# Loading the experts' weights one expert at a time in 8192-byte pieces

## The chip, the cores and the metric

The kernel runs on one core of a Trainium2 chip. A core has a matrix engine (PE), a vector engine (DVE), a scalar engine (ACT), a general engine (POOL), a queue that issues most transfers (SP) and 16 DMA engines that carry them between HBM and the on-chip memory of 128 partitions. The metric is the time of one execution in device microseconds, as a median of three runs.

## What is computed

A block of a network on 512 tokens of width 1024, all in float32: a mixer (a gated recurrence beside a spatial gating unit), and then a mixture of 32 experts of which each token takes two. The change touches the second half:

```python
mod = silu(c) @ ada_w + ada_b
sh1, sc1, g1, sh2, sc2, g2 = split(mod, 6)          # 1024 columns each
...
h = rmsnorm(x, norm2_g) * (1 + sc2) + sh2           # the second norm, modulated
g_logits = h @ w_grp + b_grp                        # 4 groups
e_logits = h @ w_exp + b_exp                        # 32 experts
# for each token the two best experts of its best group, with weights
y = (silu(h @ w1[e]) * (h @ w3[e])) @ w2[e]         # w1, w3: 1024 x 512; w2: 512 x 1024
x = rmsnorm(x + g2 * sum(weight * y), final_g)
```

The weights of 32 experts are 3 x 2 MB each, 192 MB, and every one of them is read once.

## The kernel before

The tokens lie in four tiles of 128 partitions. **The front** (to about 235 us) normalizes x, forms the modulation, runs the mixer, adds it to x (x2), turns x2 for the router's logits, ranks the tokens by expert and gathers the first ones. **The experts** are then worked through in 13 blocks of two or four experts (BLOCKS): each expert has 32 to 96 of the 128 columns of a block, and a block with two experts runs as [w1 and w3 of both, then w2 of both]. Between those products PE gathers the tokens of later blocks (lines 946 and 817), makes the one-hot matrices and adds the results of the block before to x2 (line 960).

**The modulation** comes in 12 units of 512 columns (class Ada). Units 6 to 9 are those of the second norm; each takes 256 columns of the shift and 256 of the scale, so its weights come in rows of 256 numbers, four transfers of 512 KB for a unit. unit.mm() multiplies them with silu(c), ACT copies the result from PSUM (line 208), columns() turns it into columns with four small products (line 215), and modulate() adds the bias and multiplies with the gain. Of the second norm's columns the program keeps an order of its own: x's column 256 k + 2 c + i stands in partition c of column 2 k + i. paired() is that view (every second column), parity() its other side; gain, bias and the router's weights are loaded in the same order: gain and bias into rows_b with 4-byte elements (line 260), the router's weights into wr (lines 302 and 303).

**The order of columns** has one purpose: with it a partition's rows of w1 are neighbours in memory. rows_of() gives w1 and w3 as `(k p i) f -> p k (i f)` with i = 2, that is, two rows of 512 numbers, 4096 bytes in one piece; a row of w2 has 1024 numbers, 4096 bytes too.

**The loads** are all on SP's queue in the order in which they are written. An experts' tile is 8 KB in each partition, 1 MB in all; it holds the same piece of two experts, each filled by a transfer of its own (512 KB, line 1056). The tiles stand in a ring of 12 buffers (RING: five w8, one l8, two w8q, four w8r); the first 14 loads take the buffers as the front lets them go (FIRST). A transfer waits until the buffer's last reader is done, and each transfer has one of eight semaphores in turn, so it waits as well for the transfer eight places before it. In block 0 the order is: w3, the first tile of w1, w2, two tiles of block 1's w1, the rest of w1, then the rest of block 1's w1 and its w3. Then the queue comes to a branch (line 1268) that leaves out the work for tokens that no block has room for, and goes on with block 1's w2. In the last block w2 comes in parts of 256 columns (LAST), in pieces of 1024 bytes.

**The products** of a block: up() runs k = 0 to 7 and within it the experts, so step k needs row chunk k of every expert in the block; mm() runs q = 0 to 3, both halves of the output, and the experts. In the front and in the blocks PE's order is the written one in part and a scheduler's in part; SP's is always the written one.

Of the kernel before, what the change touches and what calls it, by code (L numbers as in the profile page):

```python
# [15 lines left out]
P = 128  # L16
# [29 lines left out]
def trunk(ctx, tc, a, out):  # L46
# [132 lines left out]
    class Ada:  # L179


        def __init__(self, pieces):
            self.pieces = pieces
# [26 lines left out]
        def columns(self, second):  # L210

            ps = bank("m", (P, 4))
            for q in range(4):
                m = paired(self.m)[:, q // 2, q % 2] if second else self.m[:, q * P:(q + 1) * P]
                pe.matmul(ps[:, q:q + 1], m, quad[:, 0:1], start=True, stop=True)
            return ps
# [29 lines left out]
    unit += [Ada((3072 + 256 * q, 4096 + 256 * q)) for q in range(4)]  # L246
# [109 lines left out]
    def cg(name, k):  # L356
        return cols_g[:, off[name] + k:off[name] + k + 2]
# [34 lines left out]
    def modulate(u, q, s):  # L392
        second = s is s2c
        ps = u.columns(second)
        t = small.tile([P, 2], F32, name="modt")
        gain, shift, scale = (cg(name, 8 * i + 2 * q) if second else ca(name, 8 * i + 2 * q, 2)
                              for name, i in ((("g2n", 0), ("ada2", 0), ("ada2", 1)) if second else
                                              (("g1n", 0), ("ada", 0), ("ada", 1))))
        dve.scalar_tensor_tensor(t, ps[:, 2:4], 1.0, scale, op0=OP.add, op1=OP.add)
        dve.tensor_tensor(s[:, 1, 2 * q:2 * q + 2], ps[:, 0:2], shift, op=OP.add)  # L400
        dve.tensor_tensor(s[:, 0, 2 * q:2 * q + 2], t, gain, op=OP.mult)
# [60 lines left out]
    modulate(unit[0], 0, s1)  # L462
# [9 lines left out]
    modulate(unit[1], 1, s1)  # L472
# [4 lines left out]
    modulate(unit[2], 2, s1)  # L477
# [12 lines left out]
    modulate(unit[3], 3, s1)  # L490
# [127 lines left out]
    modulate(unit[6], 0, s2c)  # L618
# [16 lines left out]
    for k in range(KD):  # L635
        proj_step(b_u, k, ps)
        if k % 2 == 1:
            split_to(29 + k)
        if k == 1:
            unit[8].mm()  # L640
            unit[9].mm()
        if k == 4:
            modulate(unit[7], 1, s2c)
        if k == 6:
            modulate(unit[8], 2, s2c)
# [36 lines left out]
    def chunk(k):  # L682

        return slice((k % 2) * 512 + (k // 2) * P, (k % 2) * 512 + (k // 2 + 1) * P)
# [4 lines left out]
    def turned(hf, t):  # L689
# [11 lines left out]
    for k in range(KD):  # L701
# [6 lines left out]
        if k == 2:  # L708
            modulate(unit[9], 3, s2c)
# [32 lines left out]
    def logits(t, hf):  # L742
# [11 lines left out]
        act.activation(nh[:, t, :].rearrange("p (i m) -> p i m", i=2), parity(x2[:, t, :]), AF.Copy, scale=r)  # L754
# [25 lines left out]
    def parts(t, eng=None):  # L780
        for hf in range(2):
            cs = slice(hf * 512, (hf + 1) * 512)
            lo, hi = [v[:, t].rearrange("p (i h m) -> p h i m", i=2, h=2)[:, hf] for v in (nl, nh.bitcast(F32))]
# [239 lines left out]
    def rows_of(src, f):  # L1023

        i = D // f
# [4 lines left out]
    class Weights:  # L1030
# [3 lines left out]
        def __init__(self, name, b, f, cs=None, n=1):  # L1034
# [13 lines left out]
            self.todo = [(j, k) for k in range(0, self.src[0].shape[1], n) for j in range(0, len(self.src), 2)]  # L1048

        def load(self, most=2 * KD):  # L1050

            for q in range(min(most, len(self.todo))):
                j0, k = self.todo.pop(0)
                t = slot8((P, 2, self.n, self.src[0].shape[2]))
                for j in range(2):
                    sync.dma_start(t[:, j], self.src[j0 + j][:, k:k + self.n])
                    w = t[:, j] if self.cs else t[:, j].rearrange("p k (i f) -> p (k i) f", f=self.f)
                    self.r[j0 + j] += [w[:, q, :] for q in range(w.shape[1])]
# [16 lines left out]
    def block(b, along, early, before_y, after):  # L1075
# [62 lines left out]
        gT = hidden_t(gt)  # L1138
# [39 lines left out]
    def over_block(number):  # L1178
# [9 lines left out]
        def weights(src, k):  # L1188
            t = t2((P, 512))
            sync.dma_start(t, src[:, k // 2, (k % 2) * 512:(k % 2 + 1) * 512])  # L1190
# [215 lines left out]
```

## Time and profile before

| | us |
|---|---|
| median of three runs | 733.29 (731.32 to 733.75) |
| the profiled execution | 730.36 |
| its span, first to last instruction | 728.6 |
| PE busy | 678.5 (93%) |
| DVE busy | 295.6 (41%) |
| ACT busy | 174.8 (24%) |

The rows below come from the profiled execution, times in it are counted from the start of its span. An engine's busy time is the time that its instructions ran; matmuls overlap, so PE's share says little about how full it is. Of more use is the chain that ended last: it goes back from the last instruction, at each step to what released it.

### The profile page before, as it was taken

What the parts mean: (1) busy time and instruction counts of PE and PEld (TensorE: products, weight loads), DVE (VectorE), ACT (ScalarE), POOL (GpSimd) and SP (SyncE); (2) the same over time, 40 slices, a digit from 0 to 9 for tenths busy, and PEclk for the clock granted to TensorE, in tenths of its full rate; (3) what the DMA queues carried; (4) which work ended last, traced back from release to release, by engine and by line L of the source; (5) the groups of instructions that cost most, each with busy time, mean ns of one, the idle gap of its engine ahead of it and who ended that gap; (6) DMA issues with size and microseconds to landing.
All of it is one profiled execution on the core that took longest, in us unless ns stands there. A gap on an engine that the chain in (4) does not pass through costs nothing.

```text
span 728.6 us, 10224 instructions
## 1 busy us (share of the span) xinstructions
PE 678.5 (93%) x3693; PEld 358.9 (49%) x3693; DVE 295.6 (41%) x690; ACT 174.8 (24%) x317; POOL 24.4 (3%) x55
## 2 busy tenths in 40 slices
PE   8799999999998999999999999989899999989873
PEld 6467766767887435432544444333144544442131
DVE  7459439452568823311333332221123322333025
ACT  5244496342344210100110110100001110111014
POOL 3000000000103000000000000000000000000011
PEclk9899999999999999999999999999999999999997
DMA  8999606885629869999999999999999999999993
GB/s 293 287 347 319 231 1 208 274 306 208 244 78 338 346 249 409 408 409 410 408 409 409 408 410 409 409 410 408 408 410 408 409 410 408 409 404 409 361 328 118
DMA packets 99487, 246.33 MB, mean 338 GB/s; under 512 B 14072, under 2 KB 40296, under 8 KB 99432
## 3 DMA queue, kind: packets, MB, share of 16 engines
q1 hardware_dynamic: 98152, 245.09, 88.6%
q8 instruction: 30, 0.49, 0.3%
q10 hardware_dynamic: 1056, 0.52, 0.3%
q14 instruction: 25, 0.20, 0.1%
q0 software_dynamic: 224, 0.02, 0.0%
HBM read 243.51 MB, written 2.10 MB: 337 GB/s over the span
## 4 chain that ended last, share of the span: by engine, by line
DMA 60%; PE 29%; DVE 4%; SPq 3%; ACT 3%; issue 1%; POOL 0%; DVEq 0%; ACTq 0%
DMA w8r<-in_expert_w 20%; DMA w<-in_expert_w 18%; DMA l<-in_expert_w 18%; PE h L1104 4%; PE c L437 3%; PE h L437 3%; PE y L1151 3%; PE y L437 2%; PE m L204 2%; DMA w<-in_ada_w 2%; SPq L260 1%; PE h L90 1%; PE h L91 1%; PE m L946 1%; PE h L92 1%; DMA sbb<-in_sgu_b 1%
## 5 line engine op out<-in xcount | busy, mean ns | idle before, releaser
L1104 PE MATMUL h<-w,l 128*64 128x512 f32 (+1 forms) x608 | 135.5, 598 | 5.1 <-DMA w<-in_expert_w 5.0
L961 DVE TENSOR_TENSOR x<-x,c 128x512 f32<-128x512 f32 x96 | 65.9, 686 | 39.4 <-PE c L960 39.4
L1104 PEld LDWEIGHTS h<-w,l 128*64 128x64 f32 (+1 forms) x608 | 37.1, 125 | 89.5 <-issue 56.6
L1104 PE MATMUL h<-w8r,l 128*32 128x512 f32 (+1 forms) x304 | 61.9, 598 | 2.8 <-DMA w8r<-in_expert_w 2.8
L960 PE MATMUL c<-l,cT 128*128 128x512 f32 x192 | 62.4, 406 | 0.0
L946 PE MATMUL m<-l,b16h 128*128 128x256 f32 (+1 forms) x192 | 51.8, 294 | 3.2 <-ACT l L817 3.1
L1151 PE MATMUL y<-w8q,gT 128*64 128x512 f32 (+2 forms) x240 | 50.0, 570 | 3.9 <-DMA w8q<-in_expert_w 2.3
L985 DVE TENSOR_TENSOR t<-y,g2b 128x512 f32<-128x512 f32 x24 | 16.6, 692 | 89.8 <-PE y L1151 88.5
L86 ACT ACTIVATE l<-t 128x512 fp32r<-128x512 f32 (+1 forms) x35 | 21.3, 613 | 130.3 <-DVE t L985 115.7
L1151 PE MATMUL y<-w8r,gT 128*64 128x512 f32 (+2 forms) x240 | 49.3, 566 | 3.2 <-DMA w8r<-in_expert_w 3.2
L1131 DVE SCALAR_TENSOR_TENSOR t<-t,ws,h 128x512 f32<-128x512 f32 x13 | 9.7, 747 | 98.6 <-PE h L1104 98.6
L946 PE MATMUL m<-l,b16l 128*128 128x256 f32 (+1 forms) x192 | 49.1, 279 | 0.0
L817 ACT ACTIVATE l<-m,s2c 128x256 f32<-128x256 f32 (+1 forms) x24 | 13.1, 547 | 147.6 <-PE m L946 147.6
L946 PEld LDWEIGHTS m<-l,b16h 128*128 128x128 f32 x192 | 36.1, 188 | 19.6 <-ACT l L817 8.3
L242 DVE TENSOR_TENSOR w8r<-w,w8r 128x512 fp32r<-128x512 f32 x48 | 30.7, 685 | 26.6 <-ACT w8r L240 26.6
L1104 PEld LDWEIGHTS h<-w8r,l 128*32 128x32 f32 (+1 forms) x304 | 16.3, 120 | 44.8 <-issue 26.0
L946 PEld LDWEIGHTS m<-l,b16l 128*128 128x128 f32 x192 | 36.3, 189 | 2.5
L240 ACT ACTIVATE w8r<-w 128x512 fp32r<-128x512 f32 x48 | 26.9, 621 | 33.5 <-PE h L92 17.6
L1122 DVE SCALAR_TENSOR_TENSOR ws<-m,of 128x4 f32<-128x4 f32 (+1 forms) x13 | 2.1, 163 | 80.1 <-PE m L1119 80.1
L437 PE MATMUL c<-b16h,w8r 128*128 128x512 f32 x80 | 31.2, 414 | 3.1 <-ACT b16h L406 2.6
L960 PEld LDWEIGHTS c<-l,cT 128*128 128x128 f32 x192 | 29.2, 189 | 6.7 <-issue 3.4
L1114 ACT ACTIVATE t<-h 128x512 f32<-128x512 f32 x13 | 7.8, 598 | 99.4 <-PE h L1104 99.4
(358 smaller groups left out, 953.8 us busy)
## 6 DMA issues: line engine op xcount, KB each, us to landing
w<-in_expert_w SPq DMA_DIRECT2D x160, 512.0 KB, 10.1
w8r<-in_expert_w SPq DMA_DIRECT2D x124, 512.0 KB, 10.2
w8q<-in_expert_w SPq DMA_DIRECT2D x64, 512.0 KB, 10.2
l<-in_expert_w SPq DMA_DIRECT2D x36, 512.0 KB, 10.3
w<-in_ada_w SPq DMA_DIRECT2D x32, 512.0 KB, 7.5
w<-in_w_in SPq DMA_DIRECT2D x8, 1024.0 KB, 8.9
w<-in_ada_w SPq DMA_DIRECT2D x8, 1024.0 KB, 11.1
w<-in_w_out SPq DMA_DIRECT2D x4, 1024.0 KB, 8.8
```

The source lines that it names most:

```text
L86: act.activation(hi, src, AF.Copy)
L204: pe.matmul(self.ps[32 * j:32 * j + 32], cond[:, k:k + 1].to_broadcast([P, 32]), self.w[k // 4][:, j, :], start=(k < 4), stop=(k >= 4), ti ...
L240: act.activation(hi, raw, AF.Copy)
L242: return lambda: dve.tensor_tensor(lo, raw, hi.bitcast(F32), op=OP.subtract)
L437: pe.matmul(ps[c], lhs, rhs, start=(k == 0 and n == 0), stop=(k == KD - 1 and n == 2))
L817: act.activation(o, ps, AF.Identity, scale=a2[:, k:k + 1], bias=sh2[:, k:k + 1])
L946: pe.matmul(hold[k], src[:, t, chunk(k)], g[:, t, :], start=(t == 0 and i == 0), stop=(t == NT - 1 and i == 1))
L960: pe.matmul(ps, cT[:, t, :], y[:, cs], start=(i == 0), stop=(i == 1))
L961: dve.tensor_tensor(x2[:, t, cs], x2[:, t, cs], ps, op=OP.add)
L985: dve.tensor_tensor(yf, y, g2b[:, cs], op=OP.mult)
L1104: pe.matmul(h[c:c + n], xT[:, k, c:c + n], w[j][k], start=(k == 0), stop=(k == KD - 1), tile_position=(0, c))
L1151: pe.matmul(y[c:c + n], gT[:, q, c:c + n], w, start=(q == 0), stop=(q == FC - 1), tile_position=(0, c))
```

## The change

Every load of the experts' weights but the last block's w2 is one transfer of 1 MB for one expert, in pieces of 8192 bytes (four rows of w1 or w3, two of w2). So x's columns are dealt modulo 4 instead of 2: paired() and parity() take every fourth column, gain, bias and router's weights come with i = 4 (eight transfers instead of four each), and chunk() finds them in quarters. The hidden activations are turned in pairs of columns, since two rows of w2 are neighbours now (hidden_t with n = 2; n = 1 in the last block). Units 6 to 9 hold 512 columns of one kind, in the order shift, scale, shift, scale: two transfers of 1 MB each, and ACT's copy from PSUM puts the columns in order. modulate2() adds a unit's four columns of shift, or forms four of scale.

```diff
-    def paired(v):
-        return v.rearrange("p (k c i) -> p k i c", c=P, i=2)
+    def paired(v, n):
+        return v.rearrange("p (k c i) -> p k i c", c=P, i=n)
...
     def parity(v):
-        return v.rearrange("p (m i) -> p i m", i=2)
+        return v.rearrange("p (m i) -> p i m", i=4)
...
-                act.activation(self.m, self.ps, AF.Copy)
+                if self.by4:
+                    act.activation(paired(self.m, 1).rearrange("p k i c -> p (k i) c"), paired(self.ps, 4)[:, 0], AF.Copy)
+                else:
+                    act.activation(self.m, self.ps, AF.Copy)
...
-    unit += [Ada((3072 + 256 * q, 4096 + 256 * q)) for q in range(4)]
+    unit += [Ada((c,), True) for c in (3072, 4096, 3584, 4608)]
...
-        ap = ap.rearrange("(k c i) -> i k c", c=P, i=2)
-        k = 2 * ap.shape[1]
-        for i in range(2):
-            sync.dma_start(rows_b[n + i:n + k:2], ap[i])
+        ap = ap.rearrange("(k c i) -> i k c", c=P, i=4)
+        k = 4 * ap.shape[1]
+        for i in range(4):
+            sync.dma_start(rows_b[n + i:n + k:4], ap[i])
...
-    for i in range(2):
-        sync.dma_start(wr[:, i::2, 0:4], a["router_group_w"][0].rearrange("(k p i) g -> i p k g", p=P, i=2)[i])
-        sync.dma_start(wr[:, i::2, 8:40], a["router_expert_w"][0].rearrange("(k p i) g -> i p k g", p=P, i=2)[i])
+    for i in range(4):
+        sync.dma_start(wr[:, i::4, 0:4], a["router_group_w"][0].rearrange("(k p i) g -> i p k g", p=P, i=4)[i])
+        sync.dma_start(wr[:, i::4, 8:40], a["router_expert_w"][0].rearrange("(k p i) g -> i p k g", p=P, i=4)[i])
...
+    def modulate2(u, q):
+        ps = u.columns()
+        n, sl = 4 * (q // 2), slice(4 * (q // 2), 4 * (q // 2) + 4)
+        if q % 2 == 0:
+            dve.tensor_tensor(s2c[:, 1, sl], ps, cg("ada2", n), op=OP.add)
+            return
+        t = small.tile([P, 4], F32, name="modt4")
+        dve.scalar_tensor_tensor(t, ps, 1.0, cg("ada2", 8 + n), op0=OP.add, op1=OP.add)
+        dve.tensor_tensor(s2c[:, 0, sl], t, cg("g2n", n), op=OP.mult)
...
-            pe.transpose(pt[:, q, :], paired(x2[:, t])[:, k // 2, k % 2], ident)
+            pe.transpose(pt[:, q, :], paired(x2[:, t], 4)[:, k // 4, k % 4], ident)
...
-    def hidden_t(gt):
+    def hidden_t(gt, n=2):
...
-            pe.transpose(pt[:, q, :], gt[:, q * P:(q + 1) * P], ident)
+            pe.transpose(pt[:, q, :], paired(gt, n)[:, q // n, q % n], ident)
...
-        i = D // f
+        i = 2 * D // f
         return src.rearrange("e (k p i) f -> p (e k) (i f)", p=P, i=i)
...
-            self.todo = [(j, k) for k in range(0, self.src[0].shape[1], n) for j in range(0, len(self.src), 2)]
+            m = 1 if cs is None else 2
+            self.todo = [(j, k) for k in range(0, self.src[0].shape[1], n) for j in range(0, len(self.src), m)]
...
+                if self.cs is None:
+                    t = slot8((P, 2 * D))
+                    sync.dma_start(t, self.src[j][:, k])
+                    w = t.rearrange("p (i f) -> p i f", f=self.f)
+                    self.r[j] += [w[:, q, :] for q in range(w.shape[1])]
+                    continue
                 t = slot8((P, 2, self.n, self.src[0].shape[2]))
-                for j in range(2):
-                    sync.dma_start(t[:, j], self.src[j0 + j][:, k:k + self.n])
```

On SP's queue, at the start of the program, this stands behind x and the first unit's weights before (w_161 and w_164 are unit[1]'s; behind the arrow the tensor in HBM, then the shape of one transfer and how many):

```order
L232 DMA w_155<-in_w_in 128x4x512
L260 DMA rows_b<-in_norm_g 4x128x1 x2
L260 DMA rows_b<-in_ada_b 8x128x1 x2
L194 DMA w_161<-in_ada_w 128x4x256 x2
L194 DMA w_164<-in_ada_w 128x4x256 x2
```

And now (w_165 and w_168 are unit[1]'s):

```order
L234 DMA w_155<-in_w_in 128x4x512
L262 DMA rows_b<-in_norm_g 2x128x1 x4
L262 DMA rows_b<-in_ada_b 4x128x1 x4
L194 DMA w_165<-in_ada_w 128x4x256 x2
L194 DMA w_168<-in_ada_w 128x4x256 x2
```

The small transfers are eight instead of four, each with half as many rows of 128 elements; unit[1]'s come behind them as before.

On PE, the second product of block 0 before (w8q_2114 and w8q_2117 are w2's first two tiles, w8r_2120 and w8r_2123 the others; y_2560 and y_2561 the halves of the output, and each row is one matmul for either expert):

```order
L1151 MATMUL y_2560<-w8q_2114,gT_2269 64x512 x2
L1151 MATMUL y_2561<-w8q_2114,gT_2269 64x512 x2
L1151 MATMUL y_2560<-w8q_2117,gT_2269 64x512 x2
L1151 MATMUL y_2561<-w8q_2117,gT_2269 64x512 x2
L1151 MATMUL y_2560<-w8r_2120,gT_2269 64x512 x2
L1151 MATMUL y_2561<-w8r_2120,gT_2269 64x512 x2
```

The first nine of the same product now (w8q_2101 is the first tile of one expert, w8q_2103 that of the other):

```order
L1166 MATMUL y_2532<-w8q_2101,gT_2241 64x512
L1166 MATMUL y_2532<-w8q_2103,gT_2241 64x512
L1166 MATMUL y_2533<-w8q_2101,gT_2241 64x512
L1166 MATMUL y_2533<-w8q_2103,gT_2241 64x512
L1166 MATMUL y_2532<-w8q_2101,gT_2241 64x512
L1166 MATMUL y_2532<-w8q_2103,gT_2241 64x512
L1166 MATMUL y_2533<-w8q_2101,gT_2241 64x512
L1166 MATMUL y_2533<-w8q_2103,gT_2241 64x512
L1166 MATMUL y_2532<-w8r_2105,gT_2241 64x512
```

A tile was read by four matmuls of one q; now the first two tiles are read in turn over q = 0 and q = 1, and both are free behind the eighth row. (On the chip a matmul of these shapes is two instructions.)

## Rows read from the trace of the kernel before

**Rows 1.** The page: span, DMA busy tenths and GB/s in 40 slices, chain by engine.

```profile
span 728.6 us, 10224 instructions
...
DMA  8999606885629869999999999999999999999993
GB/s 293 287 347 319 231 1 208 274 306 208 244 78 338 346 249 409 408 409 410 408 409 409 408 410 409 409 410 408 408 410 408 409 410 408 409 404 409 361 328 118
...
DMA 60%; PE 29%; DVE 4%; SPq 3%; ACT 3%; issue 1%; POOL 0%; DVEq 0%; ACTq 0%
```

**Rows 2.** The chain in order of time, mid-stream: start us, us, what.

```profile
388.13 10.21 DMA w8r<-in_expert_w
...
398.36 10.22 DMA w<-in_expert_w
```

**Rows 3.** Waits of SP's queue, 296 to 640 us: total us, times, longest us.

```profile
SPq L1056 <- DMA w<-in_expert_w: 82.8, 110, 1.6
...
SPq L1056 <- PE y L1151: 3.3, 10, 0.4
```

**Rows 4.** Stretches: length, busy us of PE, PEld, DVE, ACT, POOL; clock, DMA, GB/s.

```profile
372.70:403.40 30.70, 30.50 (x256) 14.09 (x254) 10.54 (x18) 4.19 (x7) 0.00 (x0) 1.00 1.03 408
...
465.30:525.00 59.70, 53.08 (x255) 16.64 (x254) 10.54 (x18) 4.26 (x8) 0.00 (x0) 1.00 1.03 409
```

**Rows 5.** Waits, 465.3 to 525 us (block of four experts).

```profile
PEld h L1104 <- DMA w<-in_expert_w: 12.9, 14, 1.8
```

**Rows 6.** Stretches as in rows 4, loads of one piece size under way in each.

```profile
38.00:41.00 3.00, 3.00 (x22) 2.01 (x14) 0.00 (x0) 0.60 (x1) 0.00 (x0) 1.00 1.10 348
145.00:151.00 6.00, 6.00 (x34) 4.15 (x34) 0.32 (x3) 1.64 (x3) 0.00 (x0) 1.00 1.05 387
403.40:434.10 30.70, 30.50 (x162) 15.02 (x160) 10.54 (x18) 4.18 (x7) 0.00 (x0) 1.00 1.03 409
```

**Rows 7.** SP's queue in order of time: start us, us of issuing, what, how many.

```profile
9.14 8.07 SPq L260 DMA_DIRECT2D rows_b<-in_norm_g  x2
17.25 2.46 SPq L260 DMA_DIRECT2D rows_b<-in_ada_b  x2
19.76 7.49 SPq L194 DMA_DIRECT2D w<-in_ada_w  x8
```

**Rows 8.** Stretches as in rows 4, while the small transfers run.

```profile
17.90:19.15 1.25, 0.56 (x6) 0.47 (x5) 0.65 (x4) 1.18 (x3) 0.00 (x0) 1.00 0.24 2
19.15:20.30 1.15, 0.48 (x2) 0.44 (x3) 1.15 (x3) 1.15 (x2) 0.00 (x0) 1.00 0.47 3
```

**Rows 9.** PE in order of time, unit[1] and unit[7]: in brackets the wait before.

```profile
25.76 1.06 PE L204 MATMUL m<-w,cond 128*32 128x512 f32 x8 [1.34 <-DMA w<-in_ada_w]
...
120.73 1.06 PE L204 MATMUL m<-w,cond 128*32 128x512 f32 x8 [1.21 <-DMA w<-in_ada_w]
```

**Rows 10.** The chain at two sets of transposes: contiguous (L506), every second column (L695).

```profile
55.11 0.76 PE m L506 x7
...
202.65 0.47 PE m L695 x4
```

**Rows 11.** Groups by shape: count, busy us, mean ns, idle us before.

```profile
L1131 DVE SCALAR_TENSOR_TENSOR t<-t,ws,h 128x512 f32<-128x512 f32 x13 | 9.7, 747 | 98.6 <-PE h L1104 98.6
...
L789 DVE SCALAR_TENSOR_TENSOR b16l<-x,rs_r,b16h 128x512 fp32r<-128x512 f32 x6 | 4.2, 744 | 0.0
```

**Rows 12.** SP's queue around the branch.

```profile
245.42 0.80 SPq L1056 DMA_DIRECT2D l<-in_expert_w  x2
259.73 2.52 SPq L1056 DMA_DIRECT2D w8q<-in_expert_w  x4
```

**Rows 13.** PE in order of time, block 0's second product and what follows.

```profile
261.24 3.60 PE L1151 MATMUL y<-w8r,gT 128*64 128x512 f32 x16
264.67 0.60 PE L1104 MATMUL h<-w8r,l 128*64 128x512 f32 x2
```

**Rows 14.** The chain's end of the stream.

```profile
704.09 8.72 DMA w8r<-in_expert_w
```

More of the change, by code (lines that the diff above doesn't have):

```diff
@@ L179, in trunk, with __init__ @@
     class Ada:
-        def __init__(self, pieces):
-            self.pieces = pieces
+        def __init__(self, pieces, by4=False):
+            self.pieces, self.by4 = pieces, by4
         def load(self):
@@ L207, in mm, with columns @@
                 self.m = t2((P, 512))
-                act.activation(self.m, self.ps, AF.Copy)
-        def columns(self, second):
+                if self.by4:
+                    act.activation(paired(self.m, 1).rearrange("p k i c -> p (k i) c"), paired(self.ps, 4)[:, 0], AF.Copy)
+                else:
+                    act.activation(self.m, self.ps, AF.Copy)
+        def columns(self):
             ps = bank("m", (P, 4))
             for q in range(4):
-                m = paired(self.m)[:, q // 2, q % 2] if second else self.m[:, q * P:(q + 1) * P]
-                pe.matmul(ps[:, q:q + 1], m, quad[:, 0:1], start=True, stop=True)
+                pe.matmul(ps[:, q:q + 1], self.m[:, q * P:(q + 1) * P], quad[:, 0:1], start=True, stop=True)
             return ps
@@ L390, in trunk, with modulate @@
     s2c = const.tile([P, 2, KD], F32, name="s2c")
-    def modulate(u, q, s):
-        second = s is s2c
-        ps = u.columns(second)
+    def modulate(u, q):
+        ps = u.columns()
         t = small.tile([P, 2], F32, name="modt")
[L396 to L401, printed above, removed]
+        dve.scalar_tensor_tensor(t, ps[:, 2:4], 1.0, ca("ada", 8 + 2 * q, 2), op0=OP.add, op1=OP.add)
+        dve.tensor_tensor(s1[:, 1, 2 * q:2 * q + 2], ps[:, 0:2], ca("ada", 2 * q, 2), op=OP.add)
+        dve.tensor_tensor(s1[:, 0, 2 * q:2 * q + 2], t, ca("g1n", 2 * q, 2), op=OP.mult)
+    def modulate2(u, q):
+        ps = u.columns()
+        n, sl = 4 * (q // 2), slice(4 * (q // 2), 4 * (q // 2) + 4)
[5 more added lines that the diff above has]
+        dve.tensor_tensor(s2c[:, 0, sl], t, cg("g2n", n), op=OP.mult)
     def normed(k):
@@ L461, in trunk @@
     high_to(2)
-    modulate(unit[0], 0, s1)
+    modulate(unit[0], 0)
     low()
@@ L471, in trunk @@
     split_to(4)
-    modulate(unit[1], 1, s1)
+    modulate(unit[1], 1)
     normed(2)
@@ L476, in trunk @@
     proj_step(b_xr, 2, ps, (2, 3))
-    modulate(unit[2], 2, s1)
+    modulate(unit[2], 2)
     normed(4)
@@ L489, in trunk @@
     unit[3].mm()
-    modulate(unit[3], 3, s1)
+    modulate(unit[3], 3)
     normed(6)
@@ L617, in trunk @@
     rv = rstd_of(mv[:, :, 1])
-    modulate(unit[6], 0, s2c)
+    modulate2(unit[6], 0)
     yy = [[l8(F32R), l8(F32R)]]
@@ L642, in trunk @@
         if k == 4:
-            modulate(unit[7], 1, s2c)
+            modulate2(unit[7], 1)
         if k == 6:
-            modulate(unit[8], 2, s2c)
+            modulate2(unit[8], 2)
     split_to(36)
@@ L708, in trunk @@
         if k == 2:
-            modulate(unit[9], 3, s2c)
+            modulate2(unit[9], 3)
         if k == 5:
@@ L1047, in __init__ @@
             self.r = [[] for e in experts[b]]
[L1048 removed]
+            m = 1 if cs is None else 2
+            self.todo = [(j, k) for k in range(0, self.src[0].shape[1], n) for j in range(0, len(self.src), m)]
         def load(self, most=2 * KD):
             for q in range(min(most, len(self.todo))):
[L1053 removed]
+                j, k = self.todo.pop(0)
+                if self.cs is None:
[4 more added lines that the diff above has]
+                    continue
                 t = slot8((P, 2, self.n, self.src[0].shape[2]))
[L1055 to L1058 removed]
+                for i in range(2):
+                    sync.dma_start(t[:, i], self.src[j + i][:, k:k + self.n])
+                    self.r[j + i] += [t[:, i, q, :] for q in range(self.n)]
     def block_weights(b):
@@ L1137, in block @@
             u()
-        gT = hidden_t(gt)
+        gT = hidden_t(gt, 1 if last else 2)
         if b == 0:
```

10 lines of the change are left out of this document (5 added, 5 removed).

## The prediction

> **What bounds the kernel now.** I read first the slices of the span and the chain that ended last [rows 1]. From about 270 us to 690 us the DMA engines are busy all the time at 408 to 410 GB/s, and DMA makes 60% of the chain. In order of time the chain there is 38 steps of one kind [rows 2]: from the issue of one 512 KB load to its landing, about 10.22 us. The waits of the load queue say why a step is that long: between 296 and 640 us its issues wait for earlier loads to land, hardly for PE to free a buffer [rows 3]. Eight loads are under way at once, so 10.22 us is 8 x 512 KB at 410 GB/s: 1 MB, one buffer of the ring, takes 10.22 / 4 = 2.555 us. PE is not far behind: in a block of two experts it works through 30.7 us without waiting for a load, as long as the 12 buffers of that block take to arrive (12 x 2.555 = 30.7) [rows 4]. Only in a block of four experts (24 buffers, 61 us) does it stand waiting [rows 5]. Ahead of 235 us nothing is bound by the rate of the DMA engines throughout; there single late loads and then PE's own row of work set the time.
>
> **The change part by part.** The sum is made against the profiled execution, 730.36 us, of which 728.6 us are the span.
>
> *The stream of weights.* Every load of an expert's matrix but those of the last block's w2 becomes one transfer of 1 MB in 8192-byte pieces, where two transfers of 512 KB in 4096-byte pieces filled the same buffer. What a piece costs is read from three stretches in which the engines were full with pieces of one size, by the tile shapes of the loads then under way [rows 6]: 1024 bytes (unit[3]) at 348 GB/s, 2048 bytes (unit[10], unit[11]) at 387, 4096 bytes at 409. With 16 engines a piece takes size x 16 / rate: 47.1, 84.7 and 160.2 ns. The steps are 37.6 ns for the second KB and 37.75 for each of the next two, a straight line with 9.2 ns left over per piece. Carried on, 8192 bytes take 160.2 + 4 x 37.75 = 311 ns, against 320.4 for two of 4096: 0.971 of the time, so 2.482 us per buffer, 0.073 less. Of 192 buffers 20 are issued before the queue's stop at 246 us and 8 keep their short pieces; 164 lie behind it, one after another. The gain is 164 x 0.073 = 12.0 us. Bounds: the rates are rounded to 1 GB/s, and the 9.2 ns could be 7 to 12, which makes 9 to 16 us; if a piece over 4096 bytes is not carried as one, 0. A loss I exclude, since at worst the piece is the two pieces of before.
>
> [...]
>
> *The small transfers for the second norm's gain and bias.* Four transfers of 4-byte elements become eight, with the same 3072 elements. They stand on SP's queue ahead of unit[1].load() [rows 7], and while they run the engines do almost nothing else [rows 8]: one with 4 rows of 128 elements took the stretch of 1.25 us, one with 8 rows the 1.15 us behind it, at twice the busy share. So a transfer lasts as long as one row of 128, however many rows lie side by side, and after the change each has rows of 128 still, half as many. Four more cost 4 x 1.2 = 4.8 us. Behind them PE already waits for unit[1]'s weights, 1.34 us at 25.76 [rows 9], and the loads that follow are issued one after another behind these, so all of it moves. Bounds: 0 if the time follows the elements, 5.0 at the longer stretch each.
>
> *Units 6 to 9 of the modulation* come in 2048-byte pieces, two transfers instead of four. Only one of these loads ends a wait of PE, unit[7]'s second half: 1.21 us [rows 9]. Its 1 MB takes 3.0 us at 348 GB/s and 2.7 at 387: -0.3 us; bound, the whole 1.2. The other DMA time saved ahead of 235 us I count at nothing: from there to the experts no wait of PE ends with a load. That same unbroken row of PE work hides the router's four extra small transfers (about 130 us); without that cover they would cost 4 x 1.2 us.
>
> *Strided reads.* The 32 transposes of x2 read every 4th column instead of every 2nd. They lie on PE's row of work: 0.47 us for four, 118 ns each, where contiguous ones take 0.76 / 7 = 109 [rows 10]. One more doubling at the same step is 32 x 9 ns = 0.3 us; at twice their time, 3.8. The elementwise operations that read x2 with the same step (ACT's copy to nh, DVE's remainder to nl) pay nothing for every 2nd column now: 744 ns against 747 for a contiguous one of that size [rows 11]. I take 0.2 us for them, bounds 0 and 3.0 (four of the six at twice their time).
>
> [...]
>
> The smaller arithmetic (two or three DVE operations of a few columns) and the strided transposes of the hidden activations beside a bound stream are counted at nothing; there PE has the waits of [rows 5] to spare.
>
> *The restart of the stream.* After the branch in block 0 the queue's next load waits until PE has read the buffer of w2's first tile: it is issued at 259.73 us, 14 us behind the last one [rows 12], when q = 0 is done. That tile now holds one expert's rows of q = 0 and q = 1, and is free 8 instructions later; 16 of them take 264.67 - 261.24 = 3.43 us [rows 13], so 8 take 1.7. By then all loads issued ahead of the branch have long landed, so the stream starts 1.7 us later and ends so. Bounds 0 and, if the next pair's release repeats the gap, 3.4.
>
> *What stays.* In steady state a buffer is held some 1.7 us longer by PE, out of 8 loads under way, each now 2.48 us long: it is hidden. If that cover were gone, it would cost once 1.7. The last loads (1024-byte pieces) and what follows them keep their shape [rows 14].
>
> Sum: -12.0 + 4.8 - 0.3 + 0.3 + 0.2 + 1.7 = **-5.3 us**: 725.1 against 730.36. The profiled execution lies 2.9 us under the median of the three runs, 733.29, so the median goes to **728.0 us**.
>
> **The rivals.** All times are medians; below 731.1 is faster and above 735.5 slower by 0.3% (2.2 us), about what can be told from no change here.
> 1. *The stream gains nothing*: the engines cut a piece at 4096 bytes, or 409 GB/s is another limit that the line through three sizes only grazes. Then 6.7 us of costs stand alone: 740.0, slower. It decides from 2.528 us per buffer up (a gain below 4.5 us). For it: no load of before has a longer piece. Against: the straight line [rows 6].
> 2. *The share that goes is smaller*: part of the 9.2 ns isn't paid per piece. At 40% of it, 1.15% of the 320.4 ns, the stream gains 4.8 us: 733.29 - 4.8 + 6.7 = 735.2, within 0.3%. [...]
> 3. *The small transfers follow their elements*: eight take as long as four. The 4.8 us go: 723.2, faster. Against: the two stretches of [rows 8].
> 4. *PE becomes the bound*: 12 buffers arrive in 29.8 us, PE needs 30.7. If the queue had to keep its pace, the eight blocks of two experts behind the first quad would each give 0.9 us back, 7.0 in all: 735.0. Against: the lag is at most 4 x 0.9 = 3.6 us until the next block of four, in which PE waits far longer than that [rows 5], and eight transfers under way cover 20 us.
>
> **How the numbers follow.** Forecast 52%, rival 1 16%, rival 2 12%, rival 3 13%, rival 4 7%. The forecast's own range is -16 + 5 to -9 + 9, 722 to 733. Rivals 2 and 4 lie within 735; to hold 8 in 10 the range must take in rival 3's 723 and most of what lies between the forecast and rival 1, with part of the strided reads' upper bounds: **721 to 739**. What is left out is rival 1 at full cost and the thin ends. Faster: three quarters of the forecast and rival 3 (0.39 + 0.13), with 0.01 more from the others: 0.53. Within 0.3%: a fifth of the forecast and half of rivals 2 and 4: 0.20. Slower: rival 1, the other half, the forecast's rest: 0.27.
>
> **What the profile after would show.** The rate in the middle of the stream near 421 GB/s, and a chain of 8 x 1 MB steps of 19.9 us; at 409 rival 1 is right, at 414 rival 2. PE's wait for unit[1]'s first half 6.1 us instead of 1.34; as before, rival 3. The first weights after the branch issued when 16 instead of 8 instructions of that line are done. Waits for loads gone from blocks of two experts, and the queue waiting for PE there: rival 4. Transposes of 0.5 us for four; 0.9 shows the step's price. I am wrong most likely in the gain per piece, which no row of before shows at that size.

## The result, and the profile after

The changed kernel takes 722.85 us (median of 4 runs, 721.74 to 725.12); the kernel before took 733.50 beside it. The ratio is 0.987, 95% interval 0.985 to 0.990: faster by 9.5 us (7.7 to 11.1). The forecast was 728.0 in a range of 721 to 739. The profiled executions stand closer together: 725.12 us with a span of 723.3, against 730.36 and 728.6, a difference of 5.2 to 5.3 us. The point-by-point account below is made between these two; what that leaves open of the 9.5 is said at its end.

The page of after (span, DMA packets, GB/s in 40 slices, the chain by engine), beside [rows 1]:

```profile
span 723.3 us, 9703 instructions
...
GB/s 295 200 346 305 318 24 97 271 367 183 218 124 316 218 255 427 400 422 420 421 423 420 420 419 422 420 421 419 423 421 420 420 422 420 421 421 421 383 335 120
DMA packets 68827, 246.28 MB, mean 340 GB/s; under 512 B 11064, under 2 KB 29096, under 8 KB 45224
...
PE 64%; DMA 21%; DVE 5%; ACT 4%; SPq 4%; issue 1%; POOL 0%; DVEq 0%; ACTq 0%
```

The middle of the stream runs at 419 to 423 GB/s instead of 408 to 410, and 23,600 packets are not under 8 KB: a piece of 8192 bytes is carried as one. The chain has turned round, from DMA 60% and PE 29% to PE 64%. That looks like a new bound and is not one; the experiments show why.

The chain in order of time through a block of four experts (start us, us, what), beside [rows 2]:

```profile
463.05 20.43 DMA l<-in_expert_w
483.61 19.77 DMA w<-in_expert_w
503.49 19.78 DMA w8r<-in_expert_w
523.32 5.93 PE y L1166 x26
```

A step is eight loads of 1 MB, 19.78 us from issue to landing. From one step's start to the next it is 19.88 us (483.61 to 503.49), 2.485 us per buffer, where it was 10.23 / 4 = 2.557 [rows 2] and the forecast 2.482. (The 2.472 of the expectations below is 19.78 / 8, without the 0.1 us to the next issue.) Two stretches, a block of two experts and this block of four (columns as in [rows 4]; PEld is PE's weight loads), and the waits of the queue from 300 to 650 us (total us, times, longest us), beside [rows 3]:

```profile
410.90:441.50 30.60, 30.41 (x158) 14.77 (x160) 10.51 (x18) 4.17 (x7) 0.00 (x0) 1.00 1.01 420
472.10:529.20 57.10, 44.95 (x256) 15.72 (x254) 10.50 (x18) 4.18 (x7) 0.00 (x0) 0.88 1.01 421
```

```profile
SPq L1066 <- DMA w<-in_expert_w: 84.1, 53, 2.7
...
SPq L1066 <- PE y L1166: 27.6, 19, 3.2
SPq L1066 <- PE h L1119: 22.6, 22, 3.4
```

A block of two experts still takes 30.6 us, one of four 57.1 instead of 59.7. The queue now waits for PE too (27.6 and 22.6 us, before 3.3 and 1.5), yet the rate in the same blocks is 420.

Where the two traces part, from the starts of single instructions in them (us):

| mark | before | after | shift | new in this step |
|---|---|---|---|---|
| first matmul of unit[5] | 76.8 | 82.0 | +5.2 | +5.2 |
| first transpose of x2 | 186.74 | 191.01 | +4.3 | -0.9 |
| first copy to nh on ACT | 200.59 | 204.78 | +4.2 | -0.1 |
| block 0's first product | 234.86 | 242.41 | +7.55 | +3.4 |
| first load behind the branch | 259.73 | 268.19 | +8.5 | +0.9 |
| end of the last expert's product | 714.76 | 709.71 | -5.05 | -13.5 |
| end of the span | 728.56 | 723.33 | -5.2 | -0.2 |

So the front lost 7.6 us where 5.0 had been forecast, and the stream gave 13.5 where it had been 12.0.

### The profile page after: what moved, and what is told of

The parts are those of the page before. It is cut to its first block, busy times and chain, and to the rows that moved or that the text cites. A ratio compares the mean times of both kernels' runs of the same rounds, so it can differ in the third digit from the quotient of the medians.

```text
span 723.3 us, 9703 instructions
## 1 busy us (share of the span) xinstructions
PE 658.3 (91%) x3693; PEld 358.2 (50%) x3693; DVE 297.0 (41%) x684; ACT 178.1 (25%) x317; POOL 25.0 (3%) x55
## 4 chain that ended last, share of the span: by engine, by line
PE 64%; DMA 21%; DVE 5%; ACT 4%; SPq 4%; issue 1%; POOL 0%; DVEq 0%; ACTq 0%
PE h L1119 21%; PE y L1166 11%; DMA w8r<-in_expert_w 10%; PE m L955 6%; DMA w<-in_expert_w 5%; PE c L969 4%; DMA l<-in_expert_w 4%; PE c L446 4%; PE h L446 3%; PE m L204 3%; PE y L446 2%; SPq L262 2%; DMA w<-in_ada_w 2%; SPq L1072 1%; PE h L90 1%
## 5 line engine op out<-in xcount | busy, mean ns | idle before, releaser
L1119 PE MATMUL h<-w,l 128*64 128x512 f32 (+1 forms) x616 | 152.5, 615 | 11.0 <-DMA w<-in_expert_w 11.0
L1119 PEld LDWEIGHTS h<-w,l 128*64 128x64 f32 (+1 forms) x616 | 42.8, 128 | 99.3 <-issue 76.6
L1119 PE MATMUL h<-w8r,l 128*32 128x512 f32 (+1 forms) x304 | 69.8, 612 | 2.8 <-DMA w8r<-in_expert_w 2.8
L1166 PE MATMUL y<-w8q,gT 128*64 128x512 f32 (+2 forms) x240 | 55.1, 626 | 5.2 <-DMA w8q<-in_expert_w 4.5
L1166 PE MATMUL y<-w8r,gT 128*64 128x512 f32 (+2 forms) x240 | 54.1, 611 | 5.5 <-DMA w8r<-in_expert_w 5.5
L1119 PE MATMUL h<-l,l 128*64 128x512 f32 (+1 forms) x120 | 52.5, 609 | 1.5 <-DMA l<-in_expert_w 1.5
L244 DVE TENSOR_TENSOR w8r<-w,w8r 128x512 fp32r<-128x512 f32 x48 | 30.6, 683 | 34.1 <-ACT w8r L242 34.1
L1166 PEld LDWEIGHTS y<-w8r,gT 128*64 128x64 f32 (+1 forms) x240 | 15.4, 132 | 42.2 <-issue 30.0
L1119 PEld LDWEIGHTS h<-w8r,l 128*32 128x32 f32 (+1 forms) x304 | 17.8, 123 | 34.3 <-issue 28.9
```

What stands on the lines that cost most here:

```text
L244: return lambda: dve.tensor_tensor(lo, raw, hi.bitcast(F32), op=OP.subtract)
L1119: pe.matmul(h[c:c + n], xT[:, k, c:c + n], w[j][k], start=(k == 0), stop=(k == KD - 1), tile_position=(0, c))
L1166: pe.matmul(y[c:c + n], gT[:, q, c:c + n], w, start=(q == 0), stop=(q == FC - 1), tile_position=(0, c))
```

## Experiments

**What sets the rate of the stream.** Three kernels change how an expert's buffer of 1 MB is filled, and nothing else. The first cuts the pieces:

```
-                    sync.dma_start(t, self.src[j][:, k])
+                    for h in range(2):
+                        sync.dma_start(t[:, D * h:D * h + D], self.src[j][:, k, D * h:D * h + D])
```

> The changed kernel with one thing undone: each 1 MB buffer of an expert's weights is filled by two DMAs, each of 128 pieces of 4096 bytes, in the same order and places. My theory (the piece size sets the rate of the stream): the stream falls from 421 GB/s to about 409, a buffer takes 2.555 us instead of 2.472, and over 164 buffers the time rises by 13.6 us, from 722.9 to about 736.5 (734 to 738); an eight-buffer step of the chain is 20.4 us instead of 19.8. Rival (the gain is from one expert per buffer or from the order of the loads, not from the pieces): 420 GB/s and 723.

Measured: 739.56 us, ratio 1.009 (1.007 to 1.011), slower than the kernel before and 1.6 us above the range expected. It is the change without its gain, the case of rival 1, for which the prediction had 740.0. The second keeps the piece and halves the transfer, by partitions (`t[64 * h:64 * h + 64]`):

> The changed kernel, each 1 MB buffer filled by two DMAs of 64 partitions each, so 512 KB per DMA in pieces of 8192 bytes. My theory (piece size): 421 GB/s and 723 (721 to 725). Rival (what counts is the size of a DMA, or how many are issued, of which 8192-byte pieces are only the cause): 409 GB/s and 736, as with half pieces.

Measured: 1019 us (985.5 to 1038.6). Neither theory had this. The stretches of the two (length, busy us of PE, PEld, DVE, ACT, POOL, clock, DMA, GB/s), half pieces first:

```profile
475.77:537.67 61.90, 44.46 (x254) 15.39 (x252) 10.52 (x18) 4.18 (x7) 0.00 (x0) 0.94 1.03 409
```

```profile
500.00:560.00 60.00, 43.85 (x236) 18.93 (x235) 12.55 (x22) 5.31 (x9) 0.00 (x0) 0.89 1.02 228
```

With half pieces the rate is back at 409 to the digit. With 64 partitions in a row it is 228 GB/s while the DMA engines are busy all the time: each piece took nearly twice as long (8192 x 16 / 228 = 575 ns, against 311 at 421). Why, no run shows. As a test of size it was spoilt, so two more were run: the same two halves dealt to even and odd partitions (`t[h::2]`, `self.src[j][h::2, k]`), and the converse, one transfer of 1 MB in pieces of 4096 bytes:

```
-        i = 2 * D // f
+        i = D // f
...
-                    t = slot8((P, 2 * D))
-                    sync.dma_start(t, self.src[j][:, k])
+                    t = slot8((P, 2, D))
+                    sync.dma_start(t, self.src[j][:, k:k + 2])
```

> The changed kernel, each 1 MB buffer filled by two DMAs of 512 KB in pieces of 8192 bytes, one to the even and one to the odd partitions (the earlier pair, partitions 0 to 63 and 64 to 127, fell to 213 to 229 GB/s in mid-stream). My theory (the rate goes with the piece, and the fall came from which 64 partitions were written at once): about 420 GB/s in mid-stream and 723 to 727, the end of that range if the restart in block 0 is later because eight DMAs under way are now 4 MB. Rival A (the size of a DMA counts): 409 GB/s, 736 to 740. Rival B (any DMA to 64 partitions is slow): 213 to 250 GB/s and 1000 or more.

> The changed kernel, each buffer still filled by one DMA of 1 MB for one expert, but in 256 pieces of 4096 bytes (two per partition, from two places of the memory; the rows of an expert then meet the wrong columns of x, no work is left out). My theory (piece size): 409 GB/s, 2.555 us per buffer, +13.6 us: 735 to 738. Rival (the number or the size of the DMAs): 421 GB/s and 723.

Even and odd partitions: 727.92 us, ratio 0.996 (0.994 to 0.997). One transfer with 4096-byte pieces: 736.06, ratio 1.008 (1.005 to 1.010). Their blocks of four experts, in that order:

```profile
472.81:531.55 58.74, 44.38 (x254) 16.51 (x252) 10.51 (x18) 4.19 (x8) 0.00 (x0) 0.88 1.01 421
```

```profile
474.26:535.57 61.31, 46.80 (x255) 15.86 (x253) 10.51 (x18) 4.18 (x7) 0.00 (x0) 0.89 1.03 409
```

Two transfers of 512 KB keep 421 if the piece is 8192 bytes, one of 1 MB falls to 409 if it is 4096. The piece sets the rate; number and size of the transfers do not. From the first load behind the branch to the end of the last product it is 453.0 us (one transfer) and 454.9 (two) with 4096-byte pieces, 455.0 in the kernel before, 441.5 in after. The half transfers cost where the queue restarts: 443.5 us in that stretch with even and odd partitions, and the load that opens it comes 5.0 us behind the start of block 0's second product instead of 3.9.

In pairs, the piece alone is worth 11.4 to 11.5 us of that stretch (453.0 - 441.5, 454.9 - 443.5). One transfer for a buffer instead of two takes off 1.9 to 2.0 more at either piece size, with the rate unchanged. Kernels with the same stream as after lie between 440.1 and 442.7 us, so this second part is no larger than the scatter.

**Is PE the bound now?** Half of each piece is loaded, and used twice:

```
-                    t = slot8((P, 2 * D))
-                    sync.dma_start(t, self.src[j][:, k])
+                    t = slot8((P, D))
+                    sync.dma_start(t, self.src[j][:, k, 0:D])
...
-                    self.r[j] += [w[:, q, :] for q in range(w.shape[1])]
+                    self.r[j] += 2 * [w[:, q, :] for q in range(w.shape[1])]
```

> The changed kernel, but only the first half of each 8192-byte piece is loaded and used twice (half of the experts' weights is left out, PE does all its matmuls). It shows what PE needs by itself. My theory (in the changed kernel a two-expert block takes PE 30.1 to 30.7 us and the stream 12 x 2.472 = 29.7 us, so PE already sets these blocks, and the stream only the four-expert ones): two-expert blocks stay at 30 us, four-expert ones fall from 57 to about 42, the whole to about 686 (675 to 700). Rival A (the stream alone sets the time): two-expert blocks fall to 15 to 20 us, the whole to 600 or less. Rival B (PE sets everything behind the restart): above 715.

Measured: 670.9 us (one run), below the 675 to 700 expected. A block of two experts and the block of four behind it:

```profile
424.97:455.62 30.65, 30.46 (x159) 14.58 (x155) 10.56 (x19) 4.19 (x7) 0.00 (x0) 1.00 0.62 211
455.62:486.24 30.62, 30.43 (x255) 14.01 (x253) 10.51 (x18) 4.18 (x7) 0.00 (x0) 1.00 0.96 331
```

PE needs 30.6 us for either kind; my 42 for four experts was wrong. So in after a block of two has PE at its own pace (30.6, the stream would need 12 x 2.485 = 29.8), and a block of four has 24 x 2.485 = 59.6 us of stream against 30.6 of PE. The queue gets ahead by 0.8 us in each block of two, within a ring of 12 buffers, and PE catches it in the next block of four, which takes 57.1 instead of 59.6. That is why the chain runs through PE there and the rate does not fall: the sum is still set by the bytes. By that estimate PE's share becomes a loss when the surplus of a row of such blocks outgrows the ring. The kernel that follows bears this out: there a block of two takes PE 33.8 us, the queue waits for PE 175 us in all from 300 to 650 us, and the stretch from the first load behind the branch is 449.6 us instead of 441.5.

**The read with a step of 16 bytes.** Two kernels take it away. In the first the normed rows are written in x's own order and the gather's weight loads on PE take the step:

```
-        act.activation(nh[:, t, :].rearrange("p (i m) -> p i m", i=4), parity(x2[:, t, :]), AF.Copy, scale=r)
+        act.activation(nh[:, t, :], x2[:, t, :], AF.Copy, scale=r)
...
-    def chunk(k):
-        return slice((k % 4) * 256 + (k // 4) * P, (k % 4) * 256 + (k // 4 + 1) * P)
+    def chunk(v, k):
+        return paired(v, 4)[:, k // 4, k % 4]
...
-                    pe.matmul(hold[k], src[:, t, chunk(k)], g[:, t, :],
+                    pe.matmul(hold[k], chunk(src[:, t], k), g[:, t, :],
```

> The changed kernel, but the normed rows (high and low part) are written in x's own order, so ACT, DVE and POOL read without a step; the step of 16 bytes is moved into the weight loads of the gather matmuls on PE (L955 and the gather of block 0). My theory (the 16-byte step is what lengthened ACT from 1232 to 2160 ns and DVE from 744 to 1133 ns, and cost 2.5 us between 125 and 242 us; weight loads on PE take any step, as the transposes did): ACT about 1200 ns, DVE about 700 ns, weight loads still 188 ns, 720.3 (719 to 722). Rival (weight loads pay for the step too): L955's 384 weight loads grow from 188 to 260 ns or more, the gather in front of the blocks grows by some us, and the time is 723 to 727.

Measured: 740.0 us, ratio 1.011 (1.007 to 1.015): the rival, and dearer than its 723 to 727. In the second, `parity` reads contiguous quarters, and no order is made up for:

> The changed kernel, but ACT, DVE and POOL read x without a step when they make the normed rows (the columns then are not dealt as the gather expects; no work is left out). My theory (the 16-byte step is what lengthened ACT from 1232 to 2160 ns and DVE from 744 to 1133 ns, and it lies on the path that starts block 0): ACT 1150, DVE 745, block 0 starts about 2.5 us earlier, at 239.9 (+- 0.8), and the time falls by 2.5 us to 720.4. Rival (those reads lie beside other work): durations fall, block 0 starts at 242.4 as now, 722.9.

Measured: 720.72 us, ratio 0.985 (0.983 to 0.988), which alone does not tell it from after; but block 0 starts at 237.7 us instead of 242.4, more than the 2.5 expected. Groups by shape (count, busy us, mean ns): the kernel before, then after, then the step in PE's weight loads, then no step.

```profile
L754 ACT ACTIVATE b16h<-x,rs_r 128x1024 fp32r<-128x1024 f32 x4 | 4.9, 1232 | 4.0 <-DVE rs_r L331 4.0
L695 PEld LDWEIGHTS m<-ident,x 128*128 128x128 f32 x32 | 4.7, 206 | 2.6 <-DVE x L680 1.6 <-DVE rank L777 0.4 <-issue 0.2
```

```profile
L763 ACT ACTIVATE b16h<-x,rs_r 128x1024 fp32r<-128x1024 f32 x4 | 8.6, 2160 | 4.9 <-DVE rs_r L333 4.9
L798 DVE SCALAR_TENSOR_TENSOR b16l<-x,rs_r,b16h 128x512 fp32r<-128x512 f32 x6 | 6.5, 1133 | 0.0
...
L704 PEld LDWEIGHTS m<-ident,x 128*128 128x128 f32 x32 | 4.7, 208 | 3.9 <-DVE x L689 2.2 <-DVE rank L786 1.2 <-issue 0.3
...
L955 PEld LDWEIGHTS m<-l,b16h 128*128 128x128 f32 x192 | 36.3, 189 | 19.7 <-ACT l L826 8.3 <-issue 7.3 <-PE h L1119 1.7
```

```profile
L955 PEld LDWEIGHTS m<-l,b16l 128*128 128x128 f32 x192 | 62.4, 325 | 0.0
L955 PEld LDWEIGHTS m<-l,b16h 128*128 128x128 f32 x192 | 61.4, 320 | 20.0 <-ACT l L826 8.4 <-issue 7.3 <-PE h L1119 1.7
```

```profile
L763 ACT ACTIVATE b16h<-x,rs_r 128x1024 fp32r<-128x1024 f32 x4 | 4.6, 1152 | 4.0 <-DVE rs_r L333 4.0
L798 DVE SCALAR_TENSOR_TENSOR b16l<-x,rs_r,b16h 128x512 fp32r<-128x512 f32 x6 | 4.2, 747 | 0.0
```

On ACT and DVE a step of 8 bytes was nearly free (ACT 1232 ns in the kernel before, 1152 contiguous; DVE 744 [rows 11] and 747). One of 16 bytes takes 1.9 times the contiguous time on ACT and 1.5 times on DVE. From the first copy to nh until block 0 it is 34.3 us before, 37.6 after and 34.1 without the step: 3.5 us, all of it on the path (the other 1.2 us by which block 0 starts earlier lie ahead of that copy). In PE's weight loads of these rows the step makes 189 ns into 320 and a block of two experts into 33.8 us; the gather in front of block 0 grows too. The 32 transposes of x2 load with a step of 16 bytes as fast as with one of 8 (208 ns, 206 in the kernel before). But 8 bytes was no free step there: contiguous loads of that shape, for the front's transposes in the kernel before, take 141 ns (shortest, median, longest):

```profile
L506 PEld LDWEIGHTS m<-ident,t x8: 139/141/143, 54.7 to 60.3; 128*128 128x128 f32 x8
```

The transposes of the hidden activations say the same of one and the same line: contiguous before and with a step of 8 bytes now, their loads went from 141 to 202 ns (medians). So in PE's transposes the price was paid before the change, and 16 bytes cost no more than 8.

Then writing with a step (1 KB) instead of reading with one was tried, on top of the next kernel:

```
-        act.activation(nh[:, t, :].rearrange("p (i m) -> p i m", i=4), parity(x2[:, t, :]), AF.Copy, scale=r)
+        act.activation(nh[:, t, :].rearrange("p (i m) -> p m i", i=4),
+                       x2[:, t, :].rearrange("p (m i) -> p m i", i=4), AF.Copy, scale=r)
...
```

> The kernel with columns loaded in 16-byte pieces (718.5), and ACT, DVE and POOL read x in its own order and write the normed rows with a step of 1 KB, instead of reading with a step of 16 bytes; the rows come out in the same order. If steps cost only where they are read (my theory): ACT 1150 ns instead of 2160, 2.5 us less between 125 and 242 us, 716. If a written step costs as much as a read one: no change, 718.5. If more (each element written to another line): ACT 2500 ns or more and 720 to 722.

Measured: 718.43 us, ratio 0.983 (0.981 to 0.985), and the copies are as long as before:

```profile
L761 ACT ACTIVATE b16h<-x,rs_r 128x1024 fp32r<-128x1024 f32 x4 | 8.6, 2153 | 4.9 <-DVE rs_r L333 4.9
L797 DVE SCALAR_TENSOR_TENSOR b16l<-x,rs_r,b16h 128x512 fp32r<-128x512 f32 x6 | 6.5, 1118 | 0.0
```

For these two steps the price is the same on either side, and my theory that only reads pay is wrong.

**The small transfers.** First on the kernel before alone, its four split into eight with the same elements:

```
-            sync.dma_start(rows_b[n + i:n + k:2], ap[i])
+            for h in range(2):
+                m = k // 4
+                sync.dma_start(rows_b[n + i + h * 2 * m:n + i + (h + 1) * 2 * m:2], ap[i][h * m:(h + 1) * m])
```

> The kernel before, with each of its four DMAs of 4-byte elements ahead of unit[1] split in two of half the rows: eight DMAs, the same elements. My theory (each such DMA costs about 1.2 us of the queue whatever rows it has): unit[1]'s first load is issued some 4 us later than 19.76, and the time rises by about 4 us, to 1.0055 of before (1.004 to 1.007). Rival (the cost follows the elements): unit[1] issued at 19.8 to 20.5, ratio 1.000 (0.999 to 1.001).

Measured: 734.75 us, ratio 1.0045 (1.0025 to 1.0066). SP's queue in order of time in that kernel, then in after, beside [rows 7]:

```profile
9.20 10.04 SPq L262 DMA_DIRECT2D rows_b<-in_norm_g  x4
19.28 4.08 SPq L262 DMA_DIRECT2D rows_b<-in_ada_b  x4
23.41 4.53 SPq L194 DMA_DIRECT2D w<-in_ada_w  x6
```

```profile
9.51 10.19 SPq L262 DMA_DIRECT2D rows_b<-in_norm_g  x4
19.73 4.06 SPq L262 DMA_DIRECT2D rows_b<-in_ada_b  x4
23.84 4.50 SPq L194 DMA_DIRECT2D w<-in_ada_w  x6
```

unit[1] is issued 3.7 and 4.1 us later than at 19.76, and block 0 in the split kernel starts 4.2 us later. The count makes the price, not the elements. The remedy follows: the columns are loaded straight into their tile, 16 bytes to a piece, by two transfers, and no rows need be transposed.

```
-        ap = ap.rearrange("(k c i) -> i k c", c=P, i=4)
-        k = 4 * ap.shape[1]
-        for i in range(4):
-            sync.dma_start(rows_b[n + i:n + k:4], ap[i])
-        off[name] = n - 40
+        k = ap.shape[0] // P
+        sync.dma_start(cols_g[:, n:n + k].rearrange("p (k i) -> p k i", i=4),
+                       ap.rearrange("(k c i) -> c k i", c=P, i=4))
+        off[name] = n
...
-    dve.tensor_copy(cols_g, pt[:, 40:64])
```

> The changed kernel, but the columns of the second norm's gain and modulation bias are loaded straight into their tile [128, 24] by two DMAs with pieces of 16 bytes (768 pieces) at the same place of the queue, instead of eight DMAs of 4-byte elements into rows that are transposed. My theory (the small transfers ahead of unit[1] cost about 5 us): unit[1]'s first load is issued at about 18.5 us instead of 23.84, and the whole program ends 5.3 us earlier, at 717.5 (716 to 719). Rival (the queue waits at 10.87 to 17.5 us for a lane that the loads of x hold, and the loads behind it were late for another reason): unit[1] issued earlier, but unit[7] and the restart in block 0 where they are now, 723.

> The kernel with columns loaded in 16-byte pieces (718.5), with those two loads moved behind the loads of unit[3]. If they still hold up unit[1] at the place where they are (2.0 us of issue): 716.5. If the queue's wait is for a lane that a load of x holds, and passes to the next load in any order: 718.5.

Measured: 718.47 us, ratio 0.982 (0.980 to 0.984), and with the two moved behind unit[3] 716.70, ratio 0.980 (0.977 to 0.983). The queue in the first of them:

```profile
10.24 1.27 SPq L261 DMA_DIRECT2D cols_g<-in_norm_g  x1
11.56 0.71 SPq L261 DMA_DIRECT2D cols_g<-in_ada_b  x1
12.31 12.87 SPq L194 DMA_DIRECT2D w<-in_ada_w  x8
```

unit[1] is issued from 12.31 us, earlier than I had expected. Part of the old wait moves into the eight issues of unit[1] and unit[2] (12.87 us). The loads eight places before these are unit[0]'s, the mixer's first and the small ones, none of them a load of x; what each issue waits for is not shown. Block 0 starts at 234.3 and 233.5 us instead of 242.4. The two kernels cannot be told apart by their times (their intervals overlap), but both are faster than the kernel before and, by their ratios, than after.

**The restart.** Block 0 alone loads w2 in the old form (two experts in a buffer, two transfers with 4096-byte pieces):

```
-            w2 = [Weights("expert_w2", b, D)]
+            w2 = [Weights("expert_w2", b, D, old=b == 0)]
...
```

> The changed kernel, but block 0 alone loads w2 as the kernel before did (two experts in each buffer, two DMAs with pieces of 4096 bytes). My theory (the first buffer is free after 8 instead of 16 matmuls): the first load behind the branch is issued 3.0 us after PE starts block 0's second product, as in the kernel before (259.73 - 256.75), instead of 3.9 (268.19 - 264.27), and the time falls by less than 1 us. Rival (the issue waits for something else, as the branch itself): 3.9 us after it, no change.

Measured: 723.28 us (one run). PE and SP's queue in after, and in this kernel:

```profile
264.27 3.90 PE L1166 MATMUL y<-w8q,gT 128*64 128x512 f32 x16 [0.69 <-ACT gT L985]
```

```profile
268.19 1.40 SPq L1066 DMA_DIRECT2D w8q<-in_expert_w  x2
...
278.49 13.04 SPq L1066 DMA_DIRECT2D w<-in_expert_w  x5
```

```profile
262.99 3.90 PE L1173 MATMUL y<-w8q,gT 128*64 128x512 f32 x16 [0.69 <-ACT gT L985]
```

```profile
264.97 2.30 SPq L1073 DMA_DIRECT2D w8q<-in_expert_w  x2
...
277.22 0.90 SPq L1073 DMA_DIRECT2D w<-in_expert_w  x2
```

In after the load is issued when 16 matmuls are done (264.27 + 3.90 = 268.17), here after 1.98 us. The kernel before needed 2.98 for 8, since PE stood still for 0.78 us among them:

```profile
256.75 1.08 PE L1151 MATMUL y<-w8q,gT 128*64 128x512 f32 x4 [0.73 <-ACT gT L976]
258.61 2.80 PE L1151 MATMUL y<-w8q,gT 128*64 128x512 f32 x12 [0.78 <-issue]
```

So the first load comes 1.9 us later by the release, and 0.9 later than in the kernel before. But this load decides little: six loads on, those into w are issued 14.2 us behind the start of the product in either kernel (278.49 - 264.27, 277.22 - 262.99), since the queue waits for PE to have read the buffers (24.6 us in all from 258 to 300 us in after). The lead is lost there. From the start of the product to the end of the last one it is 444.6 us with the old form, 445.4 in after and 444.1 in the first kernel with 16-byte columns, so the time shows no price of the release.

## Why the prediction was right, and where it was not

- **The stream** was the right mechanism with the right size per piece: 421 GB/s and 2.485 us per buffer against 421 and 2.482. At 164 buffers that makes 164 x (2.557 - 2.485) = 11.8 us, and the pairs of kernels that differ in the piece alone gave 11.4 to 11.5, where the forecast was 12.0. The trace's 13.5 hold some 2 us more that the sum did not have. The same pairs put as much down to one transfer for a buffer instead of two, but it is no more than the scatter, and what it is made of stays open. Rivals 1 and 2 (409 and 414 GB/s) are out. No row or run shows the 40% of rival 2: at 421 GB/s a piece of 8192 bytes takes 311 ns, against 320.4 for two of 4096, 9 ns less, which is the whole 9.2 of one piece.
- **The small transfers**: forecast +4.8, +5.2 at unit[5] in the pair of traces, +4.3 where they are alone. The 0.4 between forecast and trace means nothing: in the kernels with after's front, unit[5] starts anywhere from 80.8 to 83.1 us (82.0 in after). The rule from [rows 8], a transfer lasts as long as one row, held (four more moved the issue of unit[1] by 3.7 and 4.1 us); rival 3 is out. The announced wait of 6.1 us on PE came out as 3.5 in after (6.6 in the split kernel), since in after PE came to it later, at 26.2 us (29.65 - 3.46) instead of 24.4 in the kernel before (25.76 - 1.34 [rows 9]): from 20 to 26 us its granted clock was 0.50, in the kernel before 0.72. It fell from 1.00 at 19.4 us, in a wait of PE for ACT of 2.4 us. PE's wait in after:

```profile
29.65 1.94 PE L204 MATMUL m<-w,cond 128*32 128x512 f32 x8 [3.46 <-DMA w<-in_ada_w]
```

- **Units 6 to 9**: forecast -0.3, found -0.9 from unit[5] to the transposes. This is more than scatter: that stretch is 108.9 to 109.0 us in after and in the eight other kernels with its front, 110.0 and 109.9 in the two with the old units. But the wait that the forecast went by is not the reason alone. It went from 1.21 to 0.97, and to 0.85 in the split kernel too, which keeps the old units. The rest is not traced to one operation.
- **Transposes**: forecast +0.3, measured nothing (208 ns against 206). The forecast's rise from step to step was not there: the price came whole with the step of 8 bytes (141 ns contiguous, 206 with it).
- **Strided reads**: this step failed. I took 0.2 us, from rows at a step of 8 bytes, and gave 3.0 as the most; it was 3.5. The error was to let a row at half the step stand for this one, and the bound counted DVE's operations alone, without ACT's four copies, each 0.93 us longer now (1232 to 2160 ns; DVE's six went from 744 to 1133).
- **The restart**: the release after 16 matmuls is as described and moves the first load by 1.9 (forecast 1.7); the net was +0.9, as a stall of 0.78 us of the kernel before was gone. That the stream ends as much later was not borne out: the old form brought the first load forward and the later ones not at all.
- **Rival 4** showed both of its announced signs, no waits for loads in blocks of two and the queue waiting for PE, and cost nothing, by the argument I had put against it: the lag is paid back in the next block of four. The signs were badly chosen, since they do not tell the two apart (the block of two in [rows 4] had no wait for loads before the change either); the rate in those blocks does.

Together: 5.2 - 0.9 - 0.1 + 3.4 + 0.9 - 13.5 - 0.2 = -5.2 us, the forecast's -5.3. The agreement owes something to luck: strided reads and small transfers came out 3.2 and 0.4 dearer than forecast; the stream, the units, the restart, the transposes and the end 1.5, 0.6, 0.8, 0.4 and 0.2 better.

**What stays open.** The timed runs differ by 9.5 us (the medians by 10.7) and not by 5.2, nearly twice the forecast's 5.3. The median of 722.85 is even the number of rival 3 (723.2), whose mechanism is out: the total alone would have pointed to the wrong account. The profiled execution of before was under all the runs timed beside after (731.32 to 733.75; in later comparisons its medians were 730.8 to 732.7), that of after above all its others (721.74 to 723.41). The other kernels can be set against after through their traces: its ratio should be theirs, less the difference of the spans over 732. Half pieces give 0.988, one transfer of 4096-byte pieces 0.993, even and odd partitions 0.992, no step 0.992, the three with 16-byte columns 0.992 to 0.994. That would make after 4 to 9 us faster than before; but all of it rests on the one profiled execution of after, the slowest of its four, and so leans low. The timed runs, 7.7 to 11.1 us, are the better measure; where the 4 us between trace and timed runs lie, no trace tells.

## What to carry to other kernels

In a stream bound by bytes, look at the length of the pieces first: a fixed price per piece, read off from two or three sizes in one's own trace, extrapolated well here, even past the longest piece on record (8192 bytes: 311 ns forecast, 311 at the measured 421 GB/s). But rearranging data for longer pieces moves the step into some engine's access: from 8 to 16 bytes it was a cliff on ACT and DVE (1232 to 2160 ns, 744 to 1133), PE's weight loads for transposes paid from the first step on (141 to 206 ns), and no row at half the step tells of either. And a row of tiny transfers at the head of a queue was paid by count (eight instead of four, with the same elements: 3.7 us); two transfers with all partitions side by side took the place of eight (unit[1] issued at 12.31 us instead of 23.84).

## What was not expected of the hardware

- A transfer to 64 partitions in a row moved 228 GB/s, the same bytes to every second partition 421.
- On ACT a step cost as much where it is written (2153 ns, 1 KB) as where it is read (2160 ns, 16 bytes).
- PE's weight loads for transposes take 141 ns contiguous, 206 with a step of 8 bytes and 208 with one of 16, so a step that ACT and DVE hardly feel has its full price there. The gather's loads take 189 ns contiguous and 320 with 16 bytes.
- A block of four experts costs PE what one of two does, 30.6 us, though it has twice as many matmuls (of 32 columns instead of 64).
- In after's block of four, where PE stands idle for 12.2 us (6.6 in [rows 4]), the granted clock is 0.88, before 1.00. It was 0.51 from 480.2 to 487.1 and 0.50 from 521.2 to 528.0 us, behind waits for loads of up to 2.3 us. The rate did not fall with it: 418 and 422 GB/s there, 421 over the block.
